# The last feed-forward product turned round: tokens on the partitions, and the last norm taken per token

## The chip, the cores and the metric

The kernel runs on one core of one Trainium2 chip. The metric is the device time of one execution in microseconds. A core has a matrix engine (TensorE, in the profile PE, with its weight loads listed apart as PEld), a vector engine (DVE), a scalar engine (ACT), GpSimd (POOL) and a sync engine (SP) that here mostly issues DMA transfers. Matrix products land in PSUM, eight banks of 128 partitions x 2 KB; everything else lives in SBUF.

## The reference, cut to what matters

The model is one layer of a hybrid decoder: a convolution module and a sparse attention side by side, a cross-attention, and a gated feed-forward part (SwiGLU), with a residual addition after each and a norm before each. There are 256 tokens, a model width of 1024 and a feed-forward width of 2816. The change touches only the last two lines:

```python
def rms_norm(x, g):
    y = xf * lax.rsqrt(jnp.mean(xf * xf, axis=-1, keepdims=True) + EPS)
    return (y * g.astype(jnp.float32)).astype(x.dtype)

def swiglu(h, w_in, w_out):
    a, b = jnp.split(h @ w_in, 2, axis=-1)
    return (jax.nn.silu(a) * b) @ w_out
...
        x = x + swiglu(h, ffn_in_w[l], ffn_out_w[l])
    return rms_norm(x, final_norm_g)
```

## The kernel before, in words

Activations are kept with features on the partitions: a tensor of 256 tokens x 1024 features is a tile of 128 partitions x 8 feature blocks x 256 tokens. A product has its weights as the stationary operand (128x128) and the activations as the moving operand, 256 tokens wide. To keep float32 accuracy, every operand is split into a high and a low part in the engine's faster float32 format, and each product is three matmuls: high x high, high x low, low x high (`product`, lines 147 to 149).

Weights are streamed. `half` (line 136) loads 512 KB through SP's queue into one of three buffers "w"; `split` (line 126) makes the high part on ACT (line 129) and the low part on DVE (line 131), each into one of four buffers. So SP, ACT, DVE and PE form a pipeline with a few halves of room.

Long-lived tiles share numbered slots of SBUF (`long`, "L0" to "L14"): a new tile in a slot waits until the last reader of the old one is done. PSUM is used under tags: "mm" (two banks), "s" (two), "pt" (two), "o" and "s0" (one each), eight banks in all.

The program is written in order, and a planner with a model of the times orders the instructions of each engine's queue, taking what stands earlier in the program first where several are ready. The order on each engine is then fixed. Waits between engines are put in by the framework.

The last stages, in order:

- The cross-attention's output product (`xo`), its residual addition into `x2` (slot 10, line 674), and the sums for the norm. Its inputs come from the products `xo_ps`, which read `pxh` in slot 11.
- The first feed-forward product (lines 737 to 754), 22 chunks `f0` to `f21`. The high weight meets the high and low activation side by side, 512 columns wide (line 745); the low weight meets the high activation, 256 columns wide (line 747). Banks are "mm" and "s" in turn. Each chunk's result is gated and split into `uh` and `ul`, 128 features x 256 tokens.
- The second feed-forward product `fo` (lines 761 to 771): four column blocks of 256 output features, each over 22 feature blocks, in halves of four. Weights are stationary, `uh` and `ul` move, 256 tokens wide. Each finished bank gets `x2` added by DVE (line 774), is squared by ACT (line 776), and the squares are summed elementwise over feature blocks (lines 778 and 780). All but the last two blocks are multiplied by the norm's gain on ACT (line 784).
- The last norm (lines 785 to 795). The sum over features is a sum over partitions, so it goes through PE (`rnorm`, line 224), ACT's root (line 227) and DVE's reciprocal (line 228). The factor per token then has to stand on all partitions along the free axis, so PE spreads it into a bank (`spread`, line 235) and ACT copies it to SBUF (line 787). DVE and POOL scale the eight blocks, and SP issues five output transfers (lines 790 and 795). The output has features on the partitions and is turned on the host.

`roots("roots1")` (line 757) runs a small root on ACT after the last Silu, so that ACT has the root's table loaded before the norm.

Of the kernel before, what the change touches and what calls it, by code (L numbers as in the profile page):

```python
# [10 lines left out]
AF = mybir.ActivationFunctionType  # L11
ALU = mybir.AluOpType
AX = mybir.AxisListType

P = 128
D = 1024
S = 256
NB = D // P
# [6 lines left out]
NF = D_FF // P  # L25
BUCKETS = 32
MAX_DIST = 128
EPS = 1e-6
# [19 lines left out]
PP_GMIX, PP_GX, PP_GF, PP_GO, PP_LG, PP_LB, PP_DB = (NB * i for i in range(7))  # L48
# [12 lines left out]
def tile_hybrid_block(  # L61
# [4 lines left out]
    wst: bass.AP,  # L66
    wgn: bass.AP,
    wfo: bass.AP,
    w1: bass.AP,
    pp: bass.AP,  # L70
    cp: bass.AP,
# [3 lines left out]
    nc = tc.nc  # L75
# [6 lines left out]
    def long(name, slot, shape=(P, NB, S), dt=F32):  # L82

        return sb.tile(list(shape), dt, tag=f"L{slot}", name=name)

    def longs(names, slots, dt=F32R):
        return [long(n, i, dt=dt) for n, i in zip(names, slots)]
# [6 lines left out]
    def small(name, shape, dt=F32, tag=None, bufs=1):  # L94
        return sb.tile(shape, dt, tag=tag or name, name=name, bufs=bufs)

    def bank(name):
        return mmp.tile([P, 2, S], F32, tag="mm", name=name)

    def aux(name, shape, tag, bufs):  # L100
        return axp.tile(shape, F32, tag=tag, name=name, bufs=bufs)
# [17 lines left out]
    ident = cpt[:, CP_ID:CP_ID + P]  # L119
    eps1, eps256 = eps_t[:, 0:1], eps_t[:, 1:2]  # L120

    def col(base, j):
        return ppt[:, base + j:base + j + 1]


    def split(w, shape, name):
        hi = small(f"{name}h", shape, F32R, tag="whi", bufs=4)
        lo = small(f"{name}l", shape, F32R, tag="wlo", bufs=4)
        nc.scalar.activation(hi, w, AF.Copy)  # L129
        eng = nc.gpsimd if name in EARLY else nc.vector  # L130
        eng.tensor_tensor(out=lo, in0=w, in1=f(hi[:]), op=ALU.subtract)  # L131
        return hi, lo
# [1 line left out]
    loads = []  # L134

    def half(src, name):
        n = src.shape[1]
        w = small(name, [P, n, 256], tag="w", bufs=3)
        loads.append(nc.sync.dma_start(w, src).ins)
        return split(w, [P, n, 256], name)  # L140

    def chunk(name):
        src = wst[CHUNK_AT[name]]
# [2 lines left out]
    def product(o, wh, wl, xh, xl, start, stop):  # L146
        nc.tensor.matmul(o, lhsT=wh, rhs=xh, start=start, stop=False)  # L147
        nc.tensor.matmul(o, lhsT=wh, rhs=xl, start=False, stop=False)  # L148
        nc.tensor.matmul(o, lhsT=wl, rhs=xh, start=False, stop=stop)  # L149
# [55 lines left out]
    def part(hi, lo, src):  # L205
        copy = nc.scalar.activation(hi, src, AF.Copy)
        nc.vector.tensor_tensor(out=lo, in0=src, in1=f(hi), op=ALU.subtract)  # L207
        return copy.ins
# [9 lines left out]
    def rnorm(sq, name, scale=1.0, tag="o"):  # L218

        ps = aux(f"rn_{name}", [P, 2, 2], tag, 1)  # L220
        sqs = sq if isinstance(sq, list) else [sq]
        for i, sq in enumerate(sqs):
            for tb in range(2):
                nc.tensor.matmul(ps[:, tb], lhsT=sq[:, tb * P:tb * P + P], rhs=ones[:, 0:2], start=i + tb == 0,
                                 stop=i == len(sqs) - 1 and tb == 1)
        r = small(f"r_{name}", [P, 2], tag="rnat", bufs=2)
        nc.scalar.activation(r, ps[:, :, 0], AF.Sqrt, scale=scale, bias=eps256 if scale != 1.0 else eps1)
        nc.vector.reciprocal(r, r)
        return r

    def spread(r, name, tag="o"):

        ps = aux(f"sp_{name}", [P, S], tag, 1)
        for tb in range(2):
            nc.tensor.matmul(ps[:, tb * P:tb * P + P], lhsT=r[:, tb:tb + 1].to_broadcast([P, P]), rhs=ident,
                             start=True, stop=True)
        return ps
# [10 lines left out]
    _, xt_t, sq = twin("xtsq", F32)  # L248
# [21 lines left out]
    for kb in range(NB):  # L270
        nc.vector.scalar_tensor_tensor(out=hf[:, kb], in0=xt_t[:, kb], scalar=col(PP_GMIX, kb),
                                       in1=r1, op0=ALU.mult, op1=ALU.mult)
# [11 lines left out]
    for j in range(NB):  # L284
        ps = gemm(f"u{j}", h)
        sg = small(f"sg{j}", [P, S], tag="sg", bufs=3)
# [22 lines left out]
    def taps_g(j, begin):  # L309

        y = yt[:, j:j + 2]
        for t in range(begin, TAPS):
# [7 lines left out]
            if t > begin:  # L320
# [16 lines left out]
                     start=True, stop=True)  # L337
# [22 lines left out]
    for kv, name in enumerate(("kc", "vc")):  # L360
        ps = gemm(name, h)
        for i in range(2):
# [10 lines left out]
            out=zin[:, :, :, 0:NCMP],  # L373
            in0=bass.AP(tensor=view.tensor, offset=view.offset,
                        ap=[list(view.ap[0]), [2, 16], [S, GROUPS], [16, NCMP]]),
            in1=ppt[:, PP_POS + 16 * kv:PP_POS + 16 * kv + 16].unsqueeze(2).unsqueeze(3).to_broadcast(
                [P, 16, GROUPS, NCMP]), op=ALU.add)
        z_ps = aux(f"z_ps{kv}", [P, 64], ("o", "s0")[kv], 1)
        for l in range(16):
            nc.tensor.matmul(z_ps[:HD], lhsT=w1t[:, kv, l], rhs=zin[:, l].rearrange("p g n -> p (g n)"),  # L380
                             start=l == 0, stop=l == 15)
# [4 lines left out]
        else:  # L386
# [7 lines left out]
                     start=True, stop=True)  # L394
# [6 lines left out]
    for i in range(2):  # L401
        nc.tensor.matmul(vc_ps[:, i], lhsT=zz[:, 1, i * P:i * P + P], rhs=ppt[:, PP_W2V:PP_W2V + HD],
                         start=True, stop=True)
    nc.scalar.activation(vcs, vc_ps, AF.Copy)
    hm = cpt[:, CP_HM:CP_HM + 8].unsqueeze(2).to_broadcast([P, 8, HD])
    for i in range(2):
        nc.vector.tensor_tensor(out=vcm[:, 8 * i:8 * i + 8], in0=vcs[:, i].unsqueeze(1).to_broadcast([P, 8, HD]),
                                in1=hm, op=ALU.mult)
# [3 lines left out]
    for j in range(4):  # L412
# [7 lines left out]
        for b in range(2):  # L420
            nc.vector.scalar_tensor_tensor(out=q0[b][64:128], in0=ps[0:64, b], scalar=-0.125, in1=f(q0[b][0:64]),
                                           op0=ALU.mult, op1=ALU.subtract)
            nc.vector.scalar_tensor_tensor(out=q1[b][0:64], in0=ps[64:128, b], scalar=-0.125, in1=f(q1[b][64:128]),
                                           op0=ALU.mult, op1=ALU.subtract)
# [231 lines left out]
    _, zh, zl = twin("z")  # L656
# [77 lines left out]
    rf = small("rf", [P, S], tag="vw", bufs=2)  # L734
    nc.scalar.activation(rf, spread(rnorm(acc2, "3"), "3"), AF.Copy)
    uh, ul = (longs([f"u{c}{i}" for i in range(3)], ss) for c, ss in (("h", (4, 2, 1)), ("l", (5, 3, 6))))
    for j in range(NF):
        hs = chunk(f"f{j}")
        ab = small(f"ab{j}", [P, 2, S], tag="pr", bufs=4)
        for b in range(2):  # L740

            ps = bank(f"ps_f{j}_{b}") if j % 2 == 0 else aux(f"ps_f{j}_{b}", [P, 2, S], "s", 2)
            cs = slice(b * P, b * P + P)
            for kb in range(NB):
                nc.tensor.matmul(ps, lhsT=hs[kb // 4][0][:, kb % 4, cs], rhs=fg[:, :, kb], start=kb == 0, stop=False)  # L745
            for kb in range(NB):
                nc.tensor.matmul(ps[:, 1], lhsT=hs[kb // 4][1][:, kb % 4, cs], rhs=fg[:, 0, kb], start=False, stop=kb == NB - 1)  # L747
            nc.scalar.activation(ab[:, b], ps[:, 0], AF.Copy)  # L748
            nc.vector.tensor_tensor(out=ab[:, b], in0=ps[:, 1], in1=ab[:, b], op=ALU.add)
        nc.vector.tensor_tensor(out=ab, in0=ab, in1=rf.unsqueeze(1).to_broadcast([P, 2, S]), op=ALU.mult)  # L750
        sl = small(f"sl{j}", [P, S], tag="sg", bufs=3)
        silu = nc.scalar.activation(sl, ab[:, 0], AF.Silu)  # L752
        nc.vector.tensor_tensor(out=sl, in0=sl, in1=ab[:, 1], op=ALU.mult)
        part(uh[j // 8][:, j % 8], ul[j // 8][:, j % 8], sl[:])

    with tc.issue_after(silu.ins):
        roots("roots1")
    x3 = long("x3", 0)
    acc = small("acc3", [P, S], tag="vw", bufs=2)
    parts = [acc]  # L760
    for j in range(4):
        pss = [bank(f"fo{j}_{b}")[:, 0] if j % 2 == 0 else aux(f"fo{j}_{b}", [P, S], "pt", 2) for b in range(2)]
        for k0 in range(0, NF, 4):
            n = min(4, NF - k0)
            hi, lo = half(wfo[j, :, k0:k0 + n], f"fo{j}_{k0}")
            for b in range(2):
                cs = slice(b * P, b * P + P)
                for k in range(n):
                    kb = k0 + k
                    product(pss[b], hi[:, k, cs], lo[:, k, cs], uh[kb // 8][:, kb % 8], ul[kb // 8][:, kb % 8],  # L770
                            kb == 0, kb == NF - 1)
        for b in range(2):
            k = 2 * j + b
            nc.vector.tensor_tensor(out=x3[:, k], in0=pss[b], in1=x2[:, k], op=ALU.add)
            s2 = small(f"s3_{k}", [P, S], tag="sg", bufs=3)
            nc.scalar.activation(s2, x3[:, k], AF.Square)  # L776
            if k == 0:
                nc.gpsimd.tensor_copy(acc, s2)  # L778
            elif k < 6:
                nc.vector.tensor_tensor(out=acc, in0=acc, in1=s2, op=ALU.add)  # L780
            else:
                parts.append(s2)
            if k < 6:
                nc.scalar.activation(x3[:, k], x3[:, k], AF.Copy, scale=col(PP_GO, k))
    ro = spread(rnorm(parts, "4"), "4")
    ro_sb = small("ro_sb", [P, S], tag="vw", bufs=2)
    nc.scalar.activation(ro_sb, ro, AF.Copy)
    for k in (7, 6):
        nc.vector.scalar_tensor_tensor(out=x3[:, k], in0=x3[:, k], scalar=col(PP_GO, k), in1=ro, op0=ALU.mult, op1=ALU.mult)
        nc.sync.dma_start(out[:, k], x3[:, k])  # L790
    for k in (2, 4, 0):
        ks = slice(k, k + 2)
        eng, r = (nc.gpsimd, ro_sb[:]) if k == 0 else (nc.vector, ro)
        eng.tensor_tensor(out=x3[:, ks], in0=x3[:, ks], in1=r.unsqueeze(1).to_broadcast([P, 2, S]), op=ALU.mult)
        nc.sync.dma_start(out[:, ks], x3[:, ks])


def _buckets():
# [12 lines left out]
    return res  # L811


_OUTS = [((P, NB, S), "float32")]


# [86 lines left out]
```

## Time and profile before

| what | value |
| --- | --- |
| median of three runs | 598.36 us (597.0 to 598.94) |
| profiled execution | 597.25 us |
| its span, first to last instruction | 595.5 us |
| mean granted TensorE clock | 0.984 |
| PE busy, share of the span | 94% |
| DVE, ACT, POOL busy | 75%, 64%, 30% |
| HBM read | 96.56 MB, 167 GB/s over the span |

The profile is one execution; times in it count from the span's start. A row of a group of instructions names the line of the kernel, the engine, the operation, the written and read tiles and the shapes. A row of the timeline begins with start and length. Matmuls overlap in the array: their listed length is 0.27 to 0.39 us, while the distance between their starts is what each costs. A row of a wait reads "who waited <- for whom: us in total, times, longest".

### The profile page before, as it was taken

The numbers are of one execution on the slowest core, as the hardware profiler recorded it, in microseconds if no ns is written. First come the engines' busy times: TensorE is split into PE (matmuls) and PEld (weight loads), VectorE is DVE, ScalarE is ACT, GpSimd is POOL, SyncE is SP. The second block draws the span as 40 slices with busy tenths as digits, with TensorE's granted clock in tenths as the row PEclk, the third lists the DMA queues.
The fourth block names the chain that finished last, engine by engine and source line by source line (L and its number), as shares of the span: only waits on it lengthen the run. The fifth ranks groups of instructions, "written<-read, shape, count | busy, mean of one in ns | idle before, by whom it ended". The sixth has DMA issues, their size and how long they took to land.

```text
span 595.5 us, 11133 instructions
## 1 busy us (share of the span) xinstructions
PE 561.8 (94%) x4248; PEld 531.5 (89%) x4248; DVE 447.5 (75%) x807; ACT 382.1 (64%) x712; POOL 177.8 (30%) x127
## 2 busy tenths in 40 slices
PE   8999895969899889999999999999999999999995
PEld 7889895969899889888999999998888888899995
DVE  5585798889999999977675957577877877854542
ACT  5557686377775789969844666467666566554440
POOL 0344997688799934000000300041000000000000
PEclk9999999898899999999999999999999999999998
DMA  8755568763577535321355554145556556566631
GB/s 291 244 181 176 197 179 194 200 222 105 147 232 236 194 114 187 123 85 68 126 180 188 180 166 153 66 153 182 204 176 210 179 177 210 177 176 184 191 89 70
DMA packets 34789, 101.48 MB, mean 170 GB/s; under 512 B 3632, under 2 KB 11184, under 8 KB 34480
## 3 DMA queue, kind: packets, MB, share of 16 engines
q1 hardware_dynamic: 33008, 98.67, 51.6%
q10 hardware_dynamic: 1728, 2.10, 1.3%
q8 instruction: 33, 0.54, 0.3%
q14 instruction: 20, 0.16, 0.1%
HBM read 96.56 MB, written 3.15 MB: 167 GB/s over the span
## 4 chain that ended last, share of the span: by engine, by line
PE 64%; DVE 15%; DMA 7%; issue 6%; ACT 5%; POOL 3%; DVEq 0%; SPq 0%; ACTq 0%; POOLq 0%
PE ps_f L745 14%; PE ps_f L747 7%; DVE yp L304 4%; PE fo L149 4%; PE fo L148 4%; PE fo L147 4%; DMA q<-in_wst_dram 3%; DMA k<-in_wst_dram 2%; PE ps_xq L148 1%; PE ps_pw L148 1%; PE ps_xo L148 1%; PE ps_v L149 1%; PE ps_xq L147 1%; PE ps_xq L149 1%; PE ps_xo L147 1%
## 5 line engine op out<-in xcount | busy, mean ns | idle before, releaser
L321 POOL TENSOR_TENSOR yt<-yt,vw 128x512 f32<-128x512 f32 x69 | 113.3, 1643 | 34.0 <-ACT vw L319 29.9
L319 ACT ACTIVATE vw<-vt,ppt 128x256 f32<-128x256 f32 x114 | 51.0, 499 | 23.6 <-POOL yt L321 23.2
L745 PE MATMUL ps_f<-g,f_1h 128*128 128x512 f32 x176 | 47.9, 391 | 0.0
L745 PE MATMUL ps_f<-g,f_0h 128*128 128x512 f32 x176 | 47.7, 394 | 0.0
L304 DVE SCALAR_TENSOR_TENSOR yp<-vt,ppt,yp 128x256 f32<-128x256 f32 x98 | 43.8, 479 | 0.7
L131 DVE TENSOR_TENSOR f_0l<-f,f_0h 128x1024 fp32r<-128x1024 f32 x22 | 27.5, 1249 | 21.9 <-ACT sl L752 21.0
L778 POOL COPY acc<-s 128x256 f32<-128x256 f32 x1 | 0.8, 815 | 134.2 <-ACT s L776 134.2
L745 PEld LDWEIGHTS ps_f<-g,f_1h 128*128 128x128 f32 x176 | 33.0, 188 | 7.5 <-DVE g L680 0.4
L745 PEld LDWEIGHTS ps_f<-g,f_0h 128*128 128x128 f32 x176 | 30.4, 190 | 4.1
L748 ACT ACTIVATE ab<-ps_f 128x256 f32<-128x256 f32 x44 | 16.4, 374 | 23.7 <-PE ps_f L747 23.7
L129 ACT ACTIVATE f_0h<-f 128x1024 fp32r<-128x1024 f32 x22 | 23.3, 1060 | 12.8 <-PE ps_f L745 9.7
L683 POOL COPY acc<-s_wo 128x256 f32<-128x256 f32 x1 | 0.9, 934 | 100.1 <-ACT s_wo L676 100.1
L747 PEld LDWEIGHTS ps_f<-g,f_0l 128*128 128x128 f32 x176 | 26.9, 189 | 3.3
L747 PE MATMUL ps_f<-g,f_1l 128*128 128x256 f32 x176 | 28.4, 283 | 0.0
L747 PE MATMUL ps_f<-g,f_0l 128*128 128x256 f32 x176 | 28.0, 282 | 0.0
L131 DVE TENSOR_TENSOR f_1l<-f,f_1h 128x1024 fp32r<-128x1024 f32 x22 | 26.9, 1221 | 0.7 <-ACT f_1h L129 0.7
L747 PEld LDWEIGHTS ps_f<-g,f_1l 128*128 128x128 f32 x176 | 24.3, 192 | 0.0
L129 ACT ACTIVATE f_1h<-f 128x1024 fp32r<-128x1024 f32 x22 | 23.1, 1049 | 1.2 <-DMA f<-in_wst_dram 1.1
L317 POOL TENSOR_SCALAR vw<-vt,ppt 128x256 f32<-128x256 f32 x24 | 21.5, 907 | 0.8
L147 PE MATMUL ps_u<-hh,u_0h 128*128 128x256 f32 x64 | 18.5, 289 | 2.1 <-DVE vt L288 2.1
L131 DVE TENSOR_TENSOR u_1l<-u,u_1h 128x1024 fp32r<-128x1024 f32 x8 | 14.1, 1765 | 7.3 <-ACT u_1h L129 7.3
L148 PE MATMUL ps_u<-hl,u_0h 128*128 128x256 f32 x64 | 18.2, 284 | 1.3 <-DVE hl L207 1.3
(547 smaller groups left out, 2287.7 us busy)
## 6 DMA issues: line engine op xcount, KB each, us to landing
f<-in_wst_dram SPq DMA_DIRECT2D x44, 512.0 KB, 3.8
fo<-in_wfo_dram SPq DMA_DIRECT2D x20, 512.0 KB, 3.8
u<-in_wst_dram SPq DMA_DIRECT2D x16, 512.0 KB, 4.3
q<-in_wst_dram SPq DMA_DIRECT2D x8, 512.0 KB, 6.3
ga<-in_wst_dram SPq DMA_DIRECT2D x8, 512.0 KB, 4.0
gc<-in_wst_dram SPq DMA_DIRECT2D x8, 512.0 KB, 3.7
v<-in_wst_dram SPq DMA_DIRECT2D x8, 512.0 KB, 3.7
pw<-in_wst_dram SPq DMA_DIRECT2D x8, 512.0 KB, 3.6
```

The costliest lines, as they stand in the source:

```text
L129: nc.scalar.activation(hi, w, AF.Copy)
L131: eng.tensor_tensor(out=lo, in0=w, in1=f(hi[:]), op=ALU.subtract)
L147: nc.tensor.matmul(o, lhsT=wh, rhs=xh, start=start, stop=False)
L148: nc.tensor.matmul(o, lhsT=wh, rhs=xl, start=False, stop=False)
L149: nc.tensor.matmul(o, lhsT=wl, rhs=xh, start=False, stop=stop)
L304: nc.vector.scalar_tensor_tensor(out=yt[:, k] if last else acc[:, i], in0=v, scalar=w, in1=acc[:, i], op0=ALU.mult, op1=ALU.add)
L317: nc.gpsimd.tensor_scalar(out=pr[:, i], in0=v, scalar1=w, scalar2=0.0, op0=ALU.mult, op1=ALU.add)
L319: nc.scalar.activation(pr[:, i], v, AF.Identity, scale=w, bias=col(PP_DB, j + i) if t == 0 else 0.0)
L321: nc.gpsimd.tensor_tensor(out=y, in0=y, in1=pr, op=ALU.add)
L745: nc.tensor.matmul(ps, lhsT=hs[kb // 4][0][:, kb % 4, cs], rhs=fg[:, :, kb], start=kb == 0, stop=False)
L747: nc.tensor.matmul(ps[:, 1], lhsT=hs[kb // 4][1][:, kb % 4, cs], rhs=fg[:, 0, kb], start=False, stop=kb == NB - 1)
L748: nc.scalar.activation(ab[:, b], ps[:, 0], AF.Copy)
```

## The change

The second feed-forward product changes sides. Now `uh` and `ul` are stationary, 128 features x 128 tokens, and the weights move, 512 output features wide. There are two column halves `c` and two token blocks `tb`, so four results of 128 tokens x 512 features, each of one bank. All four are held at once: "pt" (two banks), "o" and "s0". The weights come as 22 halves of 512 KB, each two feature blocks x 512 columns. The order of the three matmuls per product is high x high, high x low (both with `uh` stationary), low x high.

The residual is no longer added by DVE. `residual_first` turns `x2` into the four banks by sixteen 128x128 transposes on PE ahead of the product, which then accumulates on top. It stands in the program behind chunk `f2`.

The last norm goes by token, which is now the partition. ACT squares each bank and sums along the free axis in one instruction, with a junk output; DVE multiplies the bank by the gain into `x3`. The gain must now vary along the free axis, so a new input `gfo` holds it on all 128 partitions, 512 KB, loaded through SP's queue into slot 11 (`gf`), in the program between the norm and the `f` loop. The first half's sum, scaled and with the epsilon added, is the bias of the root, the second half's sum its input. The factor is a column, one number per partition: ACT scales column half 0, DVE half 1. The output has tokens on the partitions and leaves in four transfers of 256 KB, half 0 through ACT's queue, half 1 through SP's.

```diff
+    gfo: bass.AP,
...
     def half(src, name):
-        n = src.shape[1]
-        w = small(name, [P, n, 256], tag="w", bufs=3)
+        w = small(name, list(src.shape), tag="w", bufs=3)
...
+    def residual_first():
+
+        banks = [[aux(f"fo{c}_{tb}", [P, 512], t, n) for tb, (t, n) in enumerate(ts)]
+                 for c, ts in enumerate(((("pt", 2), ("pt", 2)), (("o", 1), ("s0", 1))))]
+        for c in range(2):
+            for tb in range(2):
+                for k in range(4):
+                    nc.tensor.matmul(banks[c][tb][:, k * P:k * P + P], lhsT=x2[:, 4 * c + k, tb * P:tb * P + P], rhs=ident,
+                                     is_transpose=True, start=k == 0, stop=False)
+        return banks
+
+    gf = long("gf", 11, (P, 2, 512))
+    nc.sync.dma_start(gf, gfo)
     for j in range(NF):
...
+        if j == 2:
+            accs = residual_first()
...
+    x3 = long("x3", 0, (P, 2, 2, 512))
+    junk = long("junk", 9, (P, 2, 2, 512))
+    ss, rr = small("ss", [P, 2, 2]), small("rr", [P, 2])
+    for c in range(2):
+        for k0 in range(0, NF, 2):
+            hi, lo = half(wfo[c, :, k0:k0 + 2], f"fo{c}_{k0}")
+            for tb in range(2):
+                ts = slice(tb * P, tb * P + P)
+                for k in range(2):
                     kb = k0 + k
-                    product(pss[b], hi[:, k, cs], lo[:, k, cs], uh[kb // 8][:, kb % 8], ul[kb // 8][:, kb % 8],
-                            kb == 0, kb == NF - 1)
...
+                    th, tl = (u[kb // 8][:, kb % 8, ts] for u in (uh, ul))
+                    nc.tensor.matmul(accs[c][tb], lhsT=th, rhs=hi[:, k], start=False, stop=False)
+                    nc.tensor.matmul(accs[c][tb], lhsT=th, rhs=lo[:, k], start=False, stop=False)
+                    nc.tensor.matmul(accs[c][tb], lhsT=tl, rhs=hi[:, k], start=False, stop=kb == NF - 1)
+        for tb in range(2):
+            nc.scalar.activation(junk[:, tb, c], accs[c][tb], AF.Square, accum_out=ss[:, tb, c:c + 1])
+            nc.vector.tensor_tensor(out=x3[:, tb, c], in0=accs[c][tb], in1=gf[:, c], op=ALU.mult)
+            if c == 0:
+
+                nc.vector.tensor_scalar(out=ss[:, tb, 0:1], in0=ss[:, tb, 0:1], scalar1=1.0 / D, scalar2=EPS,
+                                        op0=ALU.mult, op1=ALU.add)
+    for tb in range(2):
+        r = rr[:, tb:tb + 1]
+        nc.scalar.activation(r, ss[:, tb, 1:2], AF.Sqrt, scale=1.0 / D, bias=ss[:, tb, 0:1])
+        nc.vector.reciprocal(r, r)
+        for c in range(2):
+            if c == 0:
+                nc.scalar.activation(x3[:, tb, c], x3[:, tb, c], AF.Copy, scale=r)
             else:
...
+                nc.vector.tensor_scalar(out=x3[:, tb, c], in0=x3[:, tb, c], scalar1=r, scalar2=None, op0=ALU.mult)
+            (nc.scalar if c == 0 else nc.sync).dma_start(out[tb * P:tb * P + P, 512 * c:512 * c + 512], x3[:, tb, c])
```

More of the change, by code (lines that the diff above doesn't have):

```diff
@@ L136, in half @@
     def half(src, name):
-        n = src.shape[1]
-        w = small(name, [P, n, 256], tag="w", bufs=3)
+        w = small(name, list(src.shape), tag="w", bufs=3)
         loads.append(nc.sync.dma_start(w, src).ins)
-        return split(w, [P, n, 256], name)
+        return split(w, list(src.shape), name)
     def chunk(name):
@@ L754, in tile_hybrid_block @@
         part(uh[j // 8][:, j % 8], ul[j // 8][:, j % 8], sl[:])
+        if j == 2:
+            accs = residual_first()
     with tc.issue_after(silu.ins):
         roots("roots1")
[L758 to L768, printed above, removed]
-                    kb = k0 + k
-                    product(pss[b], hi[:, k, cs], lo[:, k, cs], uh[kb // 8][:, kb % 8], ul[kb // 8][:, kb % 8],
-                            kb == 0, kb == NF - 1)
[L772 to L780, printed above, removed]
-            else:
-                parts.append(s2)
-            if k < 6:
-                nc.scalar.activation(x3[:, k], x3[:, k], AF.Copy, scale=col(PP_GO, k))
@@ L785, in tile_hybrid_block @@
[L785 to L795, printed above, removed]
+    x3 = long("x3", 0, (P, 2, 2, 512))
@@ L811, in _buckets @@
     return res
-_OUTS = [((P, NB, S), "float32")]
+_OUTS = [((S, D), "float32")]
 def kernel(**inputs):
@@ L853 @@
     fo = rows(x["ffn_out_w"][0])
-    wfo = _np.stack([fo[:, :, 256 * j:256 * j + 256] for j in range(4)])
+    wfo = _np.stack([fo[:, :, 512 * c:512 * c + 512] for c in range(2)])
+    gfo = _np.broadcast_to(x["final_norm_g"].reshape(1, 2, 512), (P, 2, 512))
     w1 = x["cmp_w1"][0].reshape(2, 16, 2, HD, HD).transpose(2, 3, 0, 1, 4).reshape(P, 2, 16, HD)
@@ L886 @@
         "xt": rows(x["x"][0].T), "memt": rows(x["mem"][0].T), "wst": wst, "wgn": _np.concatenate([win[:, :, 4608:4656], _np.zeros((P, NB, P - 48), win.dtype)], axis=2),
-        "wfo": wfo, "w1": w1, "pp": pp, "cp": cp, "rel": rel,
+        "wfo": wfo, "gfo": gfo, "w1": w1, "pp": pp, "cp": cp, "rel": rel,
     }
@@ L901 @@
     got = r.results[0]["out_0_dram"]
-    return _np.ascontiguousarray(got.transpose(2, 1, 0).reshape(1, S, D))
+    return _np.ascontiguousarray(got.reshape(1, S, D))
```

## The prediction

> **What bounds the kernel now.** I read the busy shares first, then the chain of waits of the whole run, then the chain over the last ten microseconds.
>
> ```profile
> span 595.5 us, 11133 instructions
> PE 561.8 (94%) x4248; PEld 531.5 (89%) x4248; DVE 447.5 (75%) x807; ACT 382.1 (64%) x712; POOL 177.8 (30%) x127
> PE 64%; DVE 15%; DMA 7%; issue 6%; ACT 5%; POOL 3%; DVEq 0%; SPq 0%; ACTq 0%; POOLq 0%
> ```
>
> TensorE (PE) is busy 94% of the span and holds 64% of the chain. The change touches the last 10% of the run, the product with `wfo`, called `fo`, and the norm behind it, so that stretch decides. These are windows (length, then busy time and instruction count of PE, weight loads, DVE, ACT and POOL, then granted clock, DMA share, GB/s) and two timeline rows, the first and the last `fo` matmul.
>
> ```profile
> 522.70:586.30 63.60, 63.60 (x533) 63.60 (x531) 30.71 (x41) 27.82 (x40) 0.81 (x1) 1.00 0.49 145
> 522.73 0.28 PE L147 MATMUL fo<-uh,fo_0h 128*128 128x256 f32 x1
> 585.97 0.28 PE L149 MATMUL fo<-uh,fo_20l 128*128 128x256 f32 x1
> ```
>
> PE has no gap there, at clock 1.00, while DVE and ACT work less than half the time: `fo` is paced by PE issue alone. By the code it has 4 x 22 x 2 x 3 = 528 matmuls, so 63.24 / 527 = 0.120 us each, 63.36 us in all. After it comes a serial tail, the chain of waits (start, length, what):
>
> ```profile
> 586.13 0.13 PE fo L149
> 586.29 0.44 DVE x L774
> 586.75 0.42 ACT s L776
> 587.22 0.62 PE rn L224 x4
> 587.86 0.27 ACT r L227
> 588.15 0.18 DVE r L228
> 588.38 0.72 PE sp L235 x4
> 589.12 0.39 ACT ro_sb L787
> 589.54 0.48 DVE x L789
> 590.41 1.20 DVE x L794 x2
> 590.91 1.43 SPq L795 DMA_DIRECT2D out_dram<-x  x3
> L795 SPq DMA_DIRECT2D out_dram<-x x3: 399/445/447, 590.9 to 591.9; - x3
> ```
>
> The product ends at 586.26. The last arithmetic ends at 590.41 + 1.20 = 591.61, 5.35 us later; the last output is issued by 592.34, and 3.1 us more pass to the end of the span.
>
> **The change part by part.**
>
> *Product.* It becomes 2 x 22 x 2 x 3 = 264 matmuls of 512 columns. The trace has this shape in the stage before; each row of the chain is eight matmuls, of 256 and of 512 columns:
>
> ```profile
> 426.97 0.95 PE ps_f L747 x8
> 427.92 1.84 PE ps_f L745 x8
> ```
>
> That is 0.119 and 0.230 us each, with new weights for every matmul and up to eight in a row into one bank, as it will be in `fo`. So 264 x 0.230 = 60.72 us: **-2.64 us**. Halving the instructions buys little, because time follows columns: 256 more cost 0.111.
>
> The Trainium skill, "TensorE: Matmul & The Clock Gate", section "Wait — 56ns, not 53.3ns?", has a warm matmul issue every N / 2.4 GHz plus 2.5 ns, 215.7 ns for 512 columns. This trace disagrees (230 here). By the page both shapes would be shorter, and 528 matmuls of 109.2 ns against 264 of 215.7 would differ by an estimated 0.7 us: the sum would be 2.0 us less favourable (596.5). Every row of both shapes here speaks against it, so it gets no chance of its own.
>
> *Turning x2 into the banks.* Sixteen new 128x128 transposes on PE, placed behind chunk 2 of the `f` loop. PE is gapless there, so nothing covers them. A run of four transposes in the attention part, between the products around it:
>
> ```profile
> 225.35 0.60 PE L561 MATMUL pt_a<-cpt,p 128*128 128x128 f32 x4
> 225.71 0.36 PE L147 MATMUL ps_gc<-hh,gc_1h 128*128 128x256 f32 x1
> 225.91 0.28 PE L148 MATMUL ps_gc<-hl,gc_1h 128*128 128x256 f32 x1
> ```
>
> From 225.35 to 225.91 stand four transposes and one product of 0.12, so a transpose costs 0.11 with its share of the return to products: **+1.76 us** for sixteen. Bounds: 0.09 each if they all run together (1.44), and 0.09 plus 0.08 of return each if all stand alone (2.7). Their banks ("pt", "o", "s0") are not used by the `f` loop, which has "mm" and "s"; x2 is complete long before.
>
> *Work removed inside the stage.* The residual adds, squares, gain copies and sums of the first three column blocks (DVE, ACT, one POOL copy) go; they stand under PE's gapless run, so this is worth 0. The same holds for splitting the weights: the stage's bytes are unchanged, and a 512 KB half now feeds 12 x 0.230 = 2.76 us of PE instead of 24 x 0.120 = 2.88. Its split must fit in that, on each engine:
>
> ```profile
> 523.99 1.22 DVE L131 TENSOR_TENSOR fo_12l<-fo,fo_12h 128x1024 fp32r<-128x1024 f32 x1
> 525.74 1.06 ACT L129 ACTIVATE fo_16h<-fo 128x1024 fp32r<-128x1024 f32 x1 [1.22 <-PE fo L148]
> ```
>
> It does, even with the four squares and gain products of column half 0, some 1.4 us per engine, once. Were this cover gone, each half would cost at most 1.22.
>
> *The gain load.* `gf` is one more 512 KB load on SP's queue ahead of the `f` weights, into slot 11, which frees when the `xo_ps` products have read `pxh`. Queued behind it are the `f` loads; ACT and then PE wait for those.
>
> ```profile
> 385.35 0.28 PE L148 MATMUL xo_ps<-pxl,vxh 128*128 128x256 f32 x1
> 384.40 16.32 SPq L139 DMA_DIRECT2D f<-in_wst_dram  x6
> 384.00:391.00 7.00, 7.00 (x61) 7.00 (x61) 3.52 (x4) 2.72 (x3) 0.00 (x0) 1.00 0.49 159
> f<-in_wst_dram SPq DMA_DIRECT2D x44, 512.0 KB, 3.8
> 398.64 0.28 PE L149 MATMUL ps_xo<-oxh,xo_1l 128*128 128x256 f32 x1
> 398.76 2.90 PE L745 MATMUL ps_f<-g,f_0h 128*128 128x512 f32 x12
> ACT f_0h L129 <- PE ps_xo L148: 3.0, 1, 3.0
> ACT f_1h L129 <- DMA f<-in_wst_dram: 1.1, 1, 1.1
> 592.00:594.00 2.00, 0.00 (x0) 0.00 (x0) 0.00 (x0) 0.00 (x0) 0.00 (x0) 0.50 1.00 371
> ```
>
> The slot is free at about 385.6, some 1.2 us after the first `f` load issues, and the DMA engines are half idle. At the 371 GB/s of the last row 512 KB take 1.4 us. The first split waited 3.0 us for PE, not for its load, so it has room; a later one waited 1.1 us for a load and has none, but PE never stopped for it. I take **0**, the end with the DMA slack, and keep +1.4 as the other.
>
> *The tail.* The norm now sums along the free axis: Square with an accumulator, root, reciprocal, scaling; both PE passes and the spread go. Groups (line, engine, operation | busy us, mean ns | idle before):
>
> ```profile
> L206 ACT ACTIVATE pxh<-xpt 128x512 fp32r<-128x512 f32 x4 | 2.4, 597 | 1.8 <-PE xpt L719 1.7
> L535 ACT ACTIVATION_READ_ACCUMULATOR p<-p,mins 128x1 f32 x32 | 6.2, 195 | 0.0
> L674 DVE TENSOR_TENSOR x<-ps_xo,x 128x512 f32<-128x512 f32 x4 | 2.7, 683 | 1.9 <-PE ps_xo L149 1.9
> L679 ACT ACTIVATE g<-x,ppt 128x256 fp32r<-128x256 f32 x8 | 3.6, 494 | 0.0
> L206 ACT ACTIVATE uh<-sl 128x256 fp32r<-128x256 f32 x22 | 9.2, 417 | 7.7 <-DVE sl L753 7.7
> 589.54 0.87 DVE L789 SCALAR_TENSOR_TENSOR x<-x,ppt,sp 128x256 f32<-128x256 f32 x2 [1.22 <-ACT ro_sb L787]
> ```
>
> Square of 128x512 from PSUM: 0.597 plus 0.195 to read the accumulator, 0.80. Does the gain product on DVE run beside it? Both read one PSUM bank. In the last row DVE's L789 reads `sp`, not `ro_sb`, and still waits until ACT's copy out of `sp` ends. So two readers of one bank are put one after the other, and I take the gain product (0.69) behind Square. The Trainium skill, "PSUM — Partial Sum Buffer", section "PSUM bank collisions raise a hardware error ⚠️", says that software orders any two engines on one bank, reads included; the row agrees, and without that order the sum would be 0.2 us better.
>
> The second token block's chain: Square to 0.83, gain product to 1.55, reciprocal (0.18; the root, 0.27, is done beside the product) to 1.75, ACT's scaled 128x512 copy 0.70 (0.597 and the 0.08 that a column scale adds, 494 against 417) to 2.5; 2.6 with some of the first block's copy in front. Against 5.35 that is -2.75. Two queues issue the last pair at once, 0.45 instead of 0.73 after the arithmetic: -0.28. Together **-3.0 us**; the 3.1 us to the end stay. Best: no order in the bank, Square of 0.62, 1.8 us: -3.8. Worst: the first block's scaled copy sits ahead of the second's Square (+0.7) and the late megabyte crowds the write (0.8): -1.5.
>
> *Sum.* -2.64 + 1.76 + 0 - 3.0 = **-3.9 us**. The profiled execution took 597.25 (span 595.5 and 1.75 around it), so 593.35. It lies 1.1 under the median 598.36 of the three runs; carried to the median the forecast is **594.5**. All best terms give -5.0, all worst 0.0: 593.4 to 598.4. The planner that orders all instructions sees new ones and may order the `f` stage differently; no row prices that, and I allow 0.8 us either way, an estimate of half the sixteen transposes.
>
> **The rivals.**
>
> *It gives nothing that can be measured* (within 0.3%, 1.8 us, about what this measurement can tell). Transposes scattered (2.7) cancel the product's 2.64, and ACT's order leaves the tail -1.5: 598.36 - 1.4 = 597.0. For it: PE, the bound, gains only 0.9 us even as forecast. Against: the tail loses two PE passes and a spread, 1.73 us of the chain, whatever ACT does.
>
> *Slower, because `gf` blocks SP's queue.* If it is queued ahead of the first `f` load and its slot frees late, that load waits behind it. Freed only when the `xo` products end (398.64), the first half would land 3.8 us later and be split 1.06 behind that, at 403.5, where PE wants it at 398.76: 4.7 us of idle PE, and some 7 with the second half split in turn behind it (1.06 and 1.22). That is 598.36 - 3.9 + 7 = 601.5. It decides from 5.7 us of PE idle on. Against it: slot 11's last reader runs at 385.35.
>
> *More.* If the wide matmul cost only its columns, 2 x 0.111 = 0.222, the product gains 264 x 0.008 = 2.1 more: 592.4. Against: every 512-column row of the `f` stage shows 0.230.
>
> **How the numbers follow.** Forecast 0.68, nothing 0.18, slower 0.09, more 0.05. Faster is 0.73, same 0.18, slower 0.09. The range runs from 592.6 (all best, less 0.8) to 598.4 (all worst; the upper allowance is left to the slower case), which leaves out the slower case and most of "more".
>
> **What would show it.** Right: `fo` matmuls 0.230 apart, the stage near 60.7 us without a gap; sixteen transposes near chunk 2 taking 1.4 to 2.7 us; last arithmetic 2.6 us behind the last `fo` matmul, DVE's gain product starting as Square ends. Wrong: PE waiting for ACT's split or a load near 385 to 410 or in `fo`; a `fo` spacing off 0.230; ACT scaling the first token block while the second's Square waits; outputs landing over 3.1 us after issue.

## The result, and the profile after

The changed kernel takes 594.92 us (median of seven runs, 593.02 to 596.51) against 598.7 us for the kernel before (seven runs, 597.0 to 601.91): a ratio of 0.9933, 95% interval 0.9906 to 0.996, or 2.4 to 5.6 us less. The forecast was 594.5 us.

The page of the changed kernel, its busy shares and its chain by engine:

```profile
span 593.1 us, 10569 instructions
PE 559.8 (94%) x3984; PEld 519.1 (88%) x3984; DVE 448.2 (76%) x797; ACT 380.7 (64%) x706; POOL 172.7 (29%) x125
PE 64%; DVE 17%; DMA 6%; issue 6%; ACT 4%; POOL 3%; SPq 0%; ACTq 0%; POOLq 0%
```

TensorE is still the bound, with 264 matmuls and as many weight loads fewer. The product itself, as a window (length, then busy time and count of PE, PEld, DVE, ACT and POOL, clock, DMA share, GB/s), its first and last matmul, and the transposes by tile with the first and last of their starts:

```profile
527.11:587.14 60.03, 60.03 (x266) 49.37 (x264) 28.50 (x31) 24.73 (x32) 0.00 (x0) 1.00 0.52 152
527.11 0.40 PE L785 MATMUL fo<-fo_0h,uh 128*128 128x512 f32 x1
586.75 0.39 PE L787 MATMUL fo<-fo_20h,ul 128*128 128x512 f32 x1
L744 PE MATMUL fo<-cpt,x x16: 270/272/273, 402.4 to 420.8; 128*128 128x128 f32 x16
L749 SPq DMA_DIRECT2D gf<-in_gfo_dram x1: 328/328/328, 388.5 to 388.5; - x1
```

Again no gap on PE: 59.64 us for 263 distances, 0.227 us each, where the forecast had 0.230. The transposes are not all behind chunk `f2`, where the program has them. The planner put most of them, 12 of 16, into the first six microseconds of the `f` loop. The gain load went between the first and the second `f` load.

The tail, in the timeline of the changed kernel (the matmul rows left out):

```profile
585.81 0.60 ACT L789 ACTIVATE junk<-fo 128x512 f32<-128x512 f32 x1 [8.46 <-PE fo L787]
...
586.54 0.69 DVE L790 TENSOR_TENSOR x<-fo,gf 128x512 f32<-128x512 f32 x1 [7.92 <-ACT junk L789]
...
587.17 0.60 ACT L789 ACTIVATE junk<-fo 128x512 f32<-128x512 f32 x1 [0.34 <-PE fo L787]
587.33 0.49 DVE L803 TENSOR_SCALAR x<-x,rr 128x512 f32<-128x512 f32 x1
587.67 0.19 ACT L789 ACTIVATION_READ_ACCUMULATOR junk<-fo 128x1 f32 x1
587.76 0.71 ACT L801 ACTIVATE x<-x,rr 128x512 f32<-128x512 f32 x1
...
587.89 0.69 DVE L790 TENSOR_TENSOR x<-fo,gf 128x512 f32<-128x512 f32 x1
588.37 0.28 ACT L797 ACTIVATE rr<-ss 128x1 f32<-128x1 f32 x1
...
588.69 0.16 DVE L798 RECIPROCAL rr<-rr 128x1 f32<-128x1 f32 x1
588.89 0.49 DVE L803 TENSOR_SCALAR x<-x,rr 128x512 f32<-128x512 f32 x1
588.91 0.72 ACT L801 ACTIVATE x<-x,rr 128x512 f32<-128x512 f32 x1 [0.26 <-DVE rr L798]
589.66 0.35 ACTq L804 DMA_DIRECT2D out_dram<-x  x1
```

The last matmul ends at 586.75 + 0.39 = 587.14. ACT squares the second token block at 587.17; DVE's gain product of the same bank starts at 587.89, just behind it. Then ACT scales the *first* block (587.76, 0.71) before it takes the root of the second (588.37). The last arithmetic ends at 588.91 + 0.72 = 589.63, 2.49 us after the product, where it was 5.35.

So the two profiled executions differ like this, in us:

| stretch | before | after | difference |
| --- | --- | --- | --- |
| span's start to the first `f` matmul | 398.76 | 401.50 | +2.74 |
| `f` loop, to the first `fo` matmul | 123.97 | 125.61 | +1.64 |
| `fo`, to the end of the last matmul | 63.53 | 60.03 | -3.50 |
| last matmul to the last arithmetic | 5.35 | 2.49 | -2.86 |
| last arithmetic to the end of the span | 3.9 | 3.5 | -0.4 |
| span | 595.5 | 593.1 | -2.4 |

The four stretches that the change touches give -5.1 us. The opening, all that comes ahead of the `f` loop, gives 2.7 back, although PE, DVE, ACT and POOL execute the same instructions in the same order there in both kernels. Whether the change has to do with that was the main open question.

### The profile page after: what moved, and what is told of

The parts are those of the page before. It is cut to its first block, busy times and chain, and to the rows that moved or that the text cites. A ratio compares the mean times of both kernels' runs of the same rounds, so it can differ in the third digit from the quotient of the medians.

```text
span 593.1 us, 10569 instructions
## 1 busy us (share of the span) xinstructions
PE 559.8 (94%) x3984; PEld 519.1 (88%) x3984; DVE 448.2 (76%) x797; ACT 380.7 (64%) x706; POOL 172.7 (29%) x125
## 4 chain that ended last, share of the span: by engine, by line
PE 64%; DVE 17%; DMA 6%; issue 6%; ACT 4%; POOL 3%; SPq 0%; ACTq 0%; POOLq 0%
PE ps_f L758 14%; PE ps_f L760 7%; DVE yp L304 5%; PE fo L787 3%; PE fo L786 3%; PE fo L785 3%; DMA q<-in_wst_dram 3%; POOL yt L321 2%; DMA xtsq<-in_xt_dram 1%; PE ps_xq L148 1%; PE ps_xo L148 1%; PE ps_pw L148 1%; PE ps_v L149 1%; PE ps_xq L147 1%; PE ps_xq L149 1%
## 5 line engine op out<-in xcount | busy, mean ns | idle before, releaser
L762 DVE TENSOR_TENSOR ab<-ps_f,ab 128x256 f32<-128x256 f32 x44 | 18.4, 419 | 1.3 <-ACT ab L761 1.3
L147 PE MATMUL ps_u<-hh,u_1h 128*128 128x256 f32 x64 | 18.5, 289 | 0.0
```

## The experiments

**The price of the transposes.** The edit takes them away; the residual is missing from the result.

```diff
-        for c in range(2):
-            for tb in range(2):
-                for k in range(4):
-                    nc.tensor.matmul(banks[c][tb][:, k * P:k * P + P], lhsT=x2[:, 4 * c + k, tb * P:tb * P + P], rhs=ident,
-                                     is_transpose=True, start=k == 0, stop=False)
         return banks
...
-                    nc.tensor.matmul(accs[c][tb], lhsT=th, rhs=hi[:, k], start=False, stop=False)
+                    nc.tensor.matmul(accs[c][tb], lhsT=th, rhs=hi[:, k], start=kb == 0, stop=False)
```

> The changed kernel without the sixteen transposes; the residual x2 is left out of the result, and the first matmul of each bank starts it. Theory (the transposes stand bare on TensorE): the stretch from the first matmul of the f loop to the first fo matmul falls from 125.6 us in the changed kernel to 123.9 to 124.1, as before the change (123.97); fo stays at 59.9 us and the last arithmetic 2.5 us behind it; in all 1.6 us less than the changed kernel. Rival (TensorE had room for them at the start of the f loop, where the activations are still being made, and the 1.6 us more of the changed kernel's f loop are the gain load's): the stretch stays above 125.

Measured: 591.81 us, ratio to the kernel before 0.9896 (0.9872 to 0.9919). Its first matmuls of the `f` loop and of `fo`:

```profile
401.24 1.99 PE L753 MATMUL ps_f<-g,f_0h 128*128 128x512 f32 x8
525.21 0.40 PE L780 MATMUL fo<-fo_0h,uh 128*128 128x512 f32 x1
```

The loop takes 125.21 - 1.24 = 123.97 us, to the hundredth what it took before the change, though the gain load is there. So the 1.64 us are the transposes, 0.10 us each, and the idea that PE had room for them at the loop's start falls. By the ratios the whole run is 2.2 us shorter than the changed kernel (0.9896 against 0.9933) instead of the 1.6 expected; the intervals overlap, and the loop is the better measure.

**Width or side.** Each wide matmul is made as two of 256 columns; the sides stay turned.

```diff
-                    nc.tensor.matmul(accs[c][tb], lhsT=th, rhs=hi[:, k], start=False, stop=False)
...
+                    for q in (slice(0, 256), slice(256, 512)):
+                        nc.tensor.matmul(accs[c][tb][:, q], lhsT=th, rhs=hi[:, k, q], start=False, stop=False)
...
```

> The changed kernel with every 512-column matmul of fo made as two of 256 columns into the halves of the bank, each with its own weight load. Theory (the fixed part of a matmul is saved by width): 528 matmuls 0.120 us apart, fo 63.4 us as before the change, 3.5 us more than the changed kernel; f loop and tail unchanged, the whole about 2 us (fo 0, transposes +1.6, tail -3.2, near -1.6) under the kernel before. Rival (what is saved comes from the turned sides, tokens stationary, weights moving, not from the width): fo stays near 60 us.

Measured: 596.6 us, ratio 0.9975 (0.9957 to 0.9992). Its product, first and last matmul:

```profile
526.39 0.28 PE L786 MATMUL fo<-fo_0h,uh 128*128 128x256 f32 x1
589.63 0.28 PE L788 MATMUL fo<-fo_20h,ul 128*128 128x256 f32 x1
```

63.24 us for 527 distances, 0.120 each, exactly the product before the change. The whole gain of the product is width; turning the sides alone is worth nothing there. What remains against the kernel before is 1.5 us by the ratio (0.5 to 2.6 by the interval, 2.3 by the medians). The tail less the transposes, -3.2 + 1.6 = -1.6 from the stretches, fits it.

**The gain load by itself.** The kernel before, with the new input and its load, which nothing reads.

```diff
+    gf = long("gf", 11, (P, 2, 512))
+    nc.sync.dma_start(gf, gfo)
     for j in range(NF):
```

> The kernel before with only the new input and its 512 KB load into slot 11 behind the first f load; nothing reads it. Theory (the load is covered by idle DMA time, and the 2.7 us by which the changed kernel's profile is late at the start of the f loop are drift of the opening from run to run, as all engines have the same order of instructions up to there): f loop 123.9 to 124.1 us, time the same as before within 0.3%. Rival (the load delays the f weights): TensorE has gaps in the first chunks and the f loop grows by up to 1.4 us. Rival (the new input shifts the others in memory and slows the opening): the first f matmul is 2 to 3 us later than 398.8 in this run too, and the time grows by as much.

Measured: 599.03 us, ratio 0.9997 (0.9974 to 1.002). The `f` loop runs from 399.71 to 523.70, 123.99 us: the load costs nothing there, and the median doesn't move.

**The opening.** Both kernels profiled again on one chip.

> The kernel before, profiled again, for the start of its f loop. Theory (the opening drifts from run to run, whatever the kernel): the first f matmul somewhere between 398 and 404 us, as in the seven profiles of the changed kernel and its variants (400.8 to 403.8). Rival (the change makes the opening later): again near 398.8, 2 us or more ahead of them. f loop 123.9, fo 63.3, tail 5.4 in either case.

> The same once more: theory, another value between 398 and 404; rival, near 398.8 again.

> The changed kernel beside them on the same chip: theory, within the scatter of the two profiles of the kernel before on either side; rival, 2 to 3 us later than both. f loop 125.6, fo 59.9, tail 2.5.

The first `f` product by tile, with the first and last start after the durations: the kernel before twice, then the changed kernel.

```profile
L745 PE MATMUL ps_f<-g,f_0h x176: 388/395/398, 399.8 to 521.7; 128*128 128x512 f32 x176
```

```profile
L745 PE MATMUL ps_f<-g,f_0h x176: 387/396/398, 402.9 to 524.8; 128*128 128x512 f32 x176
```

```profile
L758 PE MATMUL ps_f<-g,f_0h x176: 388/395/480, 402.2 to 525.7; 128*128 128x512 f32 x176
```

The kernel before starts its `f` loop at 398.8, 399.8 and 402.9 in three profiles, and at 399.7 with the gain load; the changed kernel and its variants lie between 400.8 and 403.8 in eight. Their times follow (598.31 and 601.42 for the two new ones), while `f` loop, `fo` and tail repeat within 0.1 us. So the opening alone scatters by some 4 us, in the kernel before too. The means are 400.3 and 401.9; the ranges overlap.

The scatter arises early. The first transposes into `pt_b` start at 227.0 to 231.1 in the kernel before and with the gain load, at 228.9 to 231.6 in the other eight. From there to the `f` loop the first four take 171.8 us each, `narrow` 171.9 and the other seven 172.0 to 172.3. These 0.3 to 0.5 us go with a wait of ACT for a weight load near 369 us, which all seven have and the other five profiles have not. The same split in the kernel before and in the changed kernel:

```profile
366.19 1.06 ACT L129 ACTIVATE xo_0h<-xo 128x1024 fp32r<-128x1024 f32 x1 [0.61 <-PE ps_xq L148]
368.85 1.06 ACT L130 ACTIVATE xo_0h<-xo 128x1024 fp32r<-128x1024 f32 x1 [0.99 <-DMA xo<-in_wst_dram]
```

The gain load alone doesn't bring this wait, and `narrow` has the new input and no such wait. So why the load comes later in the seven stays open, and so does whether any of the scatter before 227 us belongs to the change.

**The tail, by its two holds.** Two things stand ahead of the last scaling: DVE's gain product behind Square in the same bank, and ACT's scaled copy of token block 0. The changed kernel again is the comparison.

> The changed kernel as it is, beside the variants of its tail. All theories: 593 to 597 us, last arithmetic 2.5 us behind the last fo matmul; the first f matmul shows how far the opening drifts from run to run (401.5 us in its first profile, 398.8 before).

Measured: 595.03 us, ratio 0.9946 (0.9925 to 0.9968), tail 2.49 as before. First edit: the gain product of column half 1 leaves the place behind Square and is joined with the scaling.

```diff
-            nc.vector.tensor_tensor(out=x3[:, tb, c], in0=accs[c][tb], in1=gf[:, c], op=ALU.mult)
             if c == 0:
+                nc.vector.tensor_tensor(out=x3[:, tb, c], in0=accs[c][tb], in1=gf[:, c], op=ALU.mult)
...
-                nc.vector.tensor_scalar(out=x3[:, tb, c], in0=x3[:, tb, c], scalar1=r, scalar2=None, op0=ALU.mult)
+                nc.vector.scalar_tensor_tensor(out=x3[:, tb, c], in0=accs[c][tb], scalar=r, in1=gf[:, c], op0=ALU.mult, op1=ALU.mult)
```

> The changed kernel with the gain product of column half 1 put behind the reciprocal and joined with the scaling (one DVE instruction from the bank). The planner then puts ACT's scaled copy of token block 0 ahead of the Square of block 1. Theory (the order on ACT sets the tail, not the gain product behind Square in the bank): Square of block 1 starts 0.5 to 0.7 us later than in the changed kernel, and the last arithmetic ends 2.5 to 2.7 us behind the last fo matmul, no gain. Rival (the two readers of the bank set it): the chain is 0.7 us shorter, 1.8 to 1.9 us.

```profile
587.12 0.39 PE L787 MATMUL fo<-fo_20h,ul 128*128 128x512 f32 x1
...
587.43 0.72 ACT L800 ACTIVATE x<-x,rr 128x512 f32<-128x512 f32 x1 [0.23 <-DVE rr L797]
...
588.06 0.58 ACT L789 ACTIVATE junk<-fo 128x512 f32<-128x512 f32 x1
...
589.29 0.75 DVE L802 SCALAR_TENSOR_TENSOR x<-fo,rr,gf 128x512 f32<-128x512 f32 x1
```

The product ends at 587.51. ACT scales block 0 first and squares block 1 only at 588.06; the end comes at 590.04, 2.53 us behind the product. Nothing is won, but the edit doesn't take the gain product away alone: the planner moved ACT's copy ahead of Square with it.

Second edit: the last four feature blocks of column half 1 are done for block 0 first, then for block 1.

```diff
+        last = [] if c == 0 else [18, 20]
+        for ks in [[k0] for k0 in range(0, NF, 2) if k0 not in last] + ([last] if last else []):
+            hs = {k0: half(wfo[c, :, k0:k0 + 2], f"fo{c}_{k0}") for k0 in ks}
             for tb in range(2):
...
```

> The changed kernel with the last four feature blocks of column half 1 done first for token block 0 and then for block 1, so that block 0 ends 2.7 us ahead of block 1 and not 1.4. Theory: ACT's copy of block 0 is out of the way, and then the gain product holds DVE's reciprocal: last arithmetic 2.2 to 2.4 us behind the last fo matmul (0.1 to 0.3 less). Rival (only ACT's order counts): 1.9 to 2.0 us.

```profile
587.77 0.39 PE L788 MATMUL fo<-fo_20h,ul 128*128 128x512 f32 x1
...
588.92 0.69 DVE L791 TENSOR_TENSOR x<-fo,gf 128x512 f32<-128x512 f32 x1 [1.43 <-ACT junk L790]
588.92 0.29 ACT L798 ACTIVATE rr<-ss 128x1 f32<-128x1 f32 x1
589.53 0.15 DVE L799 RECIPROCAL rr<-rr 128x1 f32<-128x1 f32 x1
589.71 0.72 ACT L802 ACTIVATE x<-x,rr 128x512 f32<-128x512 f32 x1 [0.50 <-DVE rr L799]
```

ACT is free now, and the root ends at 589.21, but DVE is in the gain product and takes the reciprocal at 589.53. The tail is 590.43 - 588.16 = 2.27 us.

Both edits together:

> Both edits at once: block 0 early, and the gain product of column half 1 joined with the scaling behind the reciprocal. Theory (each alone is held by the other): last arithmetic 1.9 to 2.0 us behind the last fo matmul, 0.5 us less than the changed kernel; the whole 0.5 us under it, less than its runs scatter. Rival (the last output transfers queue behind one another, so an earlier last arithmetic brings nothing): the time from the last arithmetic to the end grows from 3.5 to 4.0 us.

```profile
589.00 0.39 PE L788 MATMUL fo<-fo_20h,ul 128*128 128x512 f32 x1
...
590.15 0.29 ACT L797 ACTIVATE rr<-ss 128x1 f32<-128x1 f32 x1
590.48 0.16 DVE L798 RECIPROCAL rr<-rr 128x1 f32<-128x1 f32 x1 [1.77 <-ACT rr L797]
590.67 0.72 ACT L801 ACTIVATE x<-x,rr 128x512 f32<-128x512 f32 x1 [0.23 <-DVE rr L798]
590.68 0.75 DVE L803 SCALAR_TENSOR_TENSOR x<-fo,rr,gf 128x512 f32<-128x512 f32 x1
```

The tail is 591.43 - 589.39 = 2.04 us, 0.45 less than in the changed kernel; some 0.15 of it is lost between the last arithmetic and the end, which grew from 3.50 to 3.65. Measured: 594.55 us, ratio to the kernel before 0.9924 (0.9899 to 0.9949); beside the changed kernel's 595.03 the times can't tell 0.3 us, only the profile shows it. Each hold was in part hidden behind the other: taken alone, the first edit gave nothing and the second 0.2.

## Why the prediction was right

**Product: direction right, size too small.** The term was -2.64 us; first start to last start, the same step gives 527 x 0.120 - 263 x 0.230 = -2.75, and `fo` fell from 63.24 to 59.64, -3.60. The step that was off is "0.230 us each", read from eight matmuls of the `f` stage. Here each took 59.64 / 263 = 0.2268, and the 0.0032 between, 263 times, makes the missing 0.85. The eight are not alike, and the kernel before shows it. Here are one such eight with the matmuls behind it, and the sixth matmul of `fo` in the changed kernel:

```profile
427.76 1.09 PE L745 MATMUL ps_f<-g,f_0h 128*128 128x512 f32 x4
428.69 1.07 PE L745 MATMUL ps_f<-g,f_1h 128*128 128x512 f32 x4
429.60 0.64 PE L747 MATMUL ps_f<-g,f_0l 128*128 128x256 f32 x4
528.27 0.39 PE L787 MATMUL fo<-fo_0h,ul 128*128 128x512 f32 x1
```

From start to start the first four took 0.93 us, 0.2325 each, and the second four 0.91, 0.2275 each. Taken one by one over the loop, the first five distances behind 256-column matmuls average 0.232 and the last three 0.2267. `fo` has such a beginning only once: (528.27 - 527.11) / 5 = 0.232 for its first five distances, (586.75 - 528.27) / 258 = 0.2267 for all others. So 0.230 was the mean of five slow distances and three quick ones, carried over to 264 matmuls in a row. Why the first five take longer was not tried. The 0.222 of the rival "more" was not reached. The 215.7 ns of the Trainium skill ("TensorE: Matmul & The Clock Gate", section "Wait — 56ns, not 53.3ns?") are not borne out by this run either. The 2.0 us that the forecast estimated from that page's figures is a little high: 2.64 - 0.71 = 1.93.

**Transposes: right.** +1.76 forecast, +1.64 in the profile, and the run without them gives all of it back. They were expected behind chunk `f2`; most stood at the loop's start. The cost was nearly the same, and PE has no gap in either place that could have covered them.

**Gain load: right.** 0 forecast, 0 shown by the kernel before with the load alone. The slower rival, in which it blocks SP's queue, came true in its mechanism and not in its size. The planner put the load behind the first `f` load, and there the queue waited 1.0 us for the slot, whose last reader starts at 388.21; the load issued at 388.52. The changed kernel's wait, and the window around the start of the `f` loop:

```profile
SPq L749 <- PE xo_ps L149: 1.0, 1, 1.0
386.00:402.00 16.00, 16.00 (x136) 15.91 (x135) 11.52 (x14) 10.13 (x16) 5.18 (x5) 1.00 0.61 202
```

PE was busy for all 16 us, and for the 125.61 us of the loop behind its start, so the `f` loads behind the gain load still came in time.

**Tail: right in size, half right in its parts.** -3.0 forecast; -2.86 and -0.4 came. The gain product did start as Square ended. But the step "reciprocal ... to 1.75" took that product as what holds the chain, with 0.1 for block 0's copy. In the changed kernel the copy came between Square and root and held the root 0.5 us (587.86 to 588.37), and the gain product was done by then, at 588.58, before the root at 588.65. The chain had two holds of nearly the same length, and the forecast named the one that came second. Its total is right in part by chance: with the copy out of the way, the chain that it described took 2.27 (the second edit of the tail), where it had 2.5, and the copy that it priced at 0.1 brought that back to 2.49. The 0.2 us that it gave to the order in the bank fit: with block 0 early, taking the gain product out from between Square and the reciprocal made the tail 2.27 - 2.04 = 0.23 shorter.

**The sum.** -3.9 was forecast for all stretches and -5.1 came in them in the profiles; the median moved by 3.8. That the forecast time is so close is in part chance: the product's missing 0.9 and the opening's scatter have opposite signs. The rival that nothing measurable would come, by scattered transposes and a bad order on ACT, came true by a fraction only: the order on ACT cost 0.2 (the second edit of the tail), and the transposes nothing beyond their 1.6.

## What to carry to other kernels

Where TensorE runs without a gap, a term is a count times the distance between starts, and it is worth taking that distance to the nanosecond, start by start and not as the mean of a short group: three nanoseconds made the largest error here. Wider moving operands save only the fixed part of each matmul (2 x 0.120 against 0.227); moving a reduction from the partitions to the free axis saved nearly as much, by taking two TensorE passes and a spread out of a serial tail. In a tail shared by two engines that work in a fixed order look for the second hold before removing the first, and compare stretches of the profile, not medians, when the opening of the program scatters by more than the change.

## What the runs showed that was not expected

The time from the start to the `f` loop differed by 4 us between profiles of the same kernel (398.8 to 402.9), while everything from there to the last arithmetic, some 190 us of gapless TensorE work and its tail, repeated within 0.1 us in the three profiles of each. The granted clock may have a part in it: of 19 runs of the kernel before on one chip, the quickest (597.16 us) has a mean clock of 0.984, the highest, and the slowest (601.13 us) 0.973, the lowest, with a correlation of -0.75 over all. No run tells whether the clock is the cause.

A 128x512 scaling by a column took 0.49 us on DVE (L803) and 0.72 us on ACT (L801), so the split of the last scaling between them, one half each, leaves DVE done a quarter of a microsecond early.

The old tail had a hidden risk. In the profile of the kernel before with the gain load, the spread (L236 there) took 1.22 us and the tail 5.86 instead of 5.36. Its rows and a window around it, with the granted clock third from the end, and the like of both in the kernel before:

```profile
589.34 1.22 PE L236 MATMUL sp<-cpt,r 128*128 128x128 f32 x4 [0.55 <-DVE r L229]
590.00:591.00 1.00, 0.56 (x3) 0.27 (x2) 0.00 (x0) 0.38 (x1) 0.00 (x0) 0.50 0.00 0
```

```profile
588.38 0.71 PE L235 MATMUL sp<-cpt,r 128*128 128x128 f32 x4 [0.55 <-DVE r L228]
589.00:590.00 1.00, 0.09 (x1) 0.00 (x0) 0.46 (x2) 0.38 (x1) 0.41 (x1) 1.00 0.00 0
```

The clock had dropped to half while the spread still ran; in the kernel before it was still 1.00 when the spread ended at 589.09. The Trainium skill, "TensorE: Matmul & The Clock Gate", section "What's actually happening", says that the gate halves the clock after an idle window of some 3.4 us that runs on its own and not from the kernel's start. The trace agrees with the half (0.50) and with a moment that differs between runs. A stretch of 3.4 us shows earlier in the kernel before, at half clock between two at full clock:

```profile
140.00:143.00 3.00, 1.80 (x14) 1.54 (x14) 2.88 (x5) 2.92 (x6) 2.92 (x3) 1.00 0.08 26
143.00:146.40 3.40, 3.37 (x16) 3.40 (x16) 3.37 (x5) 2.12 (x5) 3.24 (x4) 0.50 0.40 136
146.40:150.00 3.60, 3.60 (x31) 3.60 (x31) 3.51 (x6) 1.47 (x4) 3.44 (x3) 1.00 0.63 199
```

That idle time brings the drop about no run here tests. The changed tail has no matmul, so it can't be caught by this.
